# Three later feed-forward parts: eleven chunk pairs by seven products, the last four by token blocks, and some low parts on GpSimd

## The chip, the core and the metric

The kernel runs on one core of a Trainium2 chip. TensorE (PE) multiplies, VectorE (DVE), ScalarE (ACT) and GpSimd (POOL) do the elementwise work, and SyncE (SP) issues most of the DMAs; POOL's queue issues some. The metric is the device time of one execution in microseconds (us), the median of several runs.

## The reference

Two layers over 512 tokens of width 1024. Each layer has a feed-forward part, three kinds of attention with gates (the mix), and a second feed-forward part, each followed by a layer norm:

```python
def _swiglu(x, w1, w2):
    gt, up = jnp.split(x @ w1, 2, axis=-1)
    return (jax.nn.silu(gt) * up) @ w2
...
    for l in range(DEPTH):                                   # DEPTH = 2
        x = _layer_norm(DN_ALPHA * x + 0.5 * _swiglu(x, ffn1_w1[l], ffn1_w2[l]), ln1_g[l], ln1_b[l])
        mix = _token_mix(x, w_in[l], ...)
        x = _layer_norm(DN_ALPHA * x + mix, ln2_g[l], ln2_b[l])
        x = _layer_norm(DN_ALPHA * x + 0.5 * _swiglu(x, ffn2_w1[l], ffn2_w2[l]), ln3_g[l], ln3_b[l])
    return x
```

`w1` is 1024 x 5632, `w2` is 2816 x 1024; all is float32. So there are four feed-forward parts, and the change is in their second matrix `w2`.

## The kernel before

**Split numbers.** A float32 number is held as a high part (`hi`, `sh`, `xh`: a copy in TensorE's rounded format, made by ACT) and a low part (`lo`, `sl`, `xl`: the number minus its high part, made by DVE). A product of two such numbers is three matmuls: high by high, low by high, high by low. Weights arrive by SP DMAs in `raw` buffers and are split by `wsplit` (L156).

**The second matrix, `strassen_rows` (L321).** The 2816 rows of `w2` are 22 chunks of 128 rows. Two chunks are a pair: with the two halves of the columns (512 each) and the two halves of the tokens (256 each, two blocks of 128) a pair is a product of 2 x 2 blocks, done with 7 block products where the plain way has 8. A block product is 2 token blocks x 3 matmuls of 128 x 128 by 128 x 512. Nine pairs (`NS` = 9) are done so; the last four chunks (`NTAIL`) are plain, 24 matmuls each.

- *First pass:* for each pair four of the seven products, with sums of weight blocks that the POOL queue's DMAs have added up in DRAM long before (`weight_sums`, L478, one step at a time by `sums_step`, L497: a small POOL copy that waits for a tile, then a DMA). The operands' sums of token blocks are made by DVE on the way. All eight PSUM banks accumulate.
- *Between:* ACT and DVE read the four results (`reads`, L377), and DVE adds them into the residual rows `xa` in twelve small steps (`merge`, L385), some from SBUF alone, some with an operand in PSUM.
- *Second pass:* for each pair the other three products. `second(p)` (L414) prepares a pair two ahead: the row of weights (`wrows`), the weights' sum for two pairs at a time, and `sp(p, True)` (L765), which makes `sh` (ACT) and `sl` (DVE, 128 x 768, L590) from the sums of tokens. Four such pairs of buffers exist, and five units of split weights.
- *Tail, `norm_tail` (L261):* the four plain chunks' 96 matmuls token block by token block; after each block its layer norm (`LN.steps`, L222): DVE takes the accumulators (L229), ACT the sum of squares (L232), POOL two one-column steps (L235, L236), DVE the two scalings (L234, L240). `LN.second` (L244) transposes the block and splits it for the next stage. In between the next stage's first weights are loaded and split. The next stage (`staged`, L464, or `value_rows`, L820) starts with the blocks that are done first.

PE, POOL, ACT and DVE run these stages in the order in which they are written. In the last part there is no next stage; L242 sends the result out.

Of the kernel before, what the change touches and what calls it, by code (L numbers as in the profile page):

```python
# [18 lines left out]
P = 128  # L19
# [45 lines left out]
def body(tc, a, out, depth=DEPTH):  # L65
# [89 lines left out]

    def wsplit(raw, n=KD, step=None):  # L156
        hi, lo = unit()
        step = step or n
        for i in range(0, n, step):
            c = slice(i, i + step)  # L160
            nc.scalar.activation(hi[:, c], raw[:, c], AF.Copy)  # L161
            nc.vector.tensor_tensor(lo[:, c], raw[:, c], hi[:, c].bitcast(F32), op=OP.subtract)  # L162
        return hi, lo

    def wcols(w, c0, step=None):

        r = wraw()
        nc.sync.dma_start(r, w.rearrange("(k p) f -> p k f", p=P)[:, :, c0:c0 + P])
        return wsplit(r, step=step)

# [29 lines left out]
    class LN:  # L200
# [20 lines left out]

        def steps(self, acc, tb, tpl):  # L222
            x = self.xa[tb]
            st = stats[tb]
            junk = tpl.tile([P, D], BF, name="junk", bufs=2)
            u = tpl.tile([P, D], F32, name="u", bufs=2)
            hs = [slice(0, 512), slice(512, 1024)]
            for hf, c in enumerate(hs):
                nc.vector.scalar_tensor_tensor(x[:, c], acc[hf], self.scale, x[:, c], op0=OP.mult, op1=OP.add,  # L229
                                               accum_out=st[:, hf:hf + 1])  # L230
# [3 lines left out]
            nc.vector.scalar_tensor_tensor(u, x, st[:, 2:3], self.G, op0=OP.add, op1=OP.mult)  # L234
            nc.gpsimd.tensor_scalar(st[:, 4:5], st[:, 3:4], 1.0 / D, EPS / ALPHA ** 2, op0=OP.mult, op1=OP.add)  # L235
            nc.gpsimd.tensor_tensor(st[:, 5:6], st[:, 4:5], mhalf, op=OP.pow)  # L236
            yield
            for c in hs:
                y = u if self.last else x
                nc.vector.scalar_tensor_tensor(y[:, c], u[:, c], st[:, 5:6], self.B[:, c], op0=OP.mult, op1=OP.add)  # L240
                if self.last:
                    nc.sync.dma_start(out[tb * P:(tb + 1) * P, c], y[:, c])  # L242
# [17 lines left out]

    def norm_tail(accs, half, ln, nxt, early=False):  # L261


        wts = []

        def load(n):
            for _ in range(n if nxt else 0):
                wts.append(nxt(len(wts)))

        when = [2, 1, 1, 0, 0] if early else [1, 1, 1, 0, 1]  # L270
        load(when.pop(0))
        for tb in range(NB):
            half(tb, 0)
            if tb >= 2:
                ln.second(tb - 2)
            half(tb, 1)
            if tb == NB - 1:
                next(st, 0)
            st = ln.steps(accs[tb], tb, nx.pool)
            next(st)  # L280
            next(st)
            if tb != NB - 2:
                next(st, 0)
            load(when.pop(0))
        return wts, {0: lambda: ln.second(NB - 2), 2: lambda: ln.second(NB - 1)}

# [34 lines left out]
    def strassen_rows(w2, ts, first, order, enter, sp, plain, clear, nxt, tmp, early):  # L321
# [48 lines left out]
        p1, p6, p7, p5 = (a1[i:i + 2] for i in (0, 4, 2, 6))  # L370
        a2 = acc8()
        accs = [[a2[4 * (tb // 2) + 2 * hf + tb % 2] for hf in range(2)] for tb in range(NB)]
        tt, stt = nc.vector.tensor_tensor, nc.vector.scalar_tensor_tensor
# [11 lines left out]
        def merge(b):  # L385
# [6 lines left out]
            yield stt(xb[:, c1], u3[b], -sc, xb[:, c1], op0=OP.mult, op1=OP.add)  # L392
# [18 lines left out]

        merges = chain([merge(0), merge(1)])

        def second(p):  # L414
            if p < NS:
                ready.append((weights(p), sp(p, True)))
# [3 lines left out]
        second(1)  # L420
        for p in range(NS):
            (uc, d, dc), (sh, sl) = ready.popleft()
            prods = [(0, 1, uc, lo4), (1, 0, uc, hi4), (2, 2, d, dc)]
            for i, j, w, c in prods[2:] + prods[:2] if p and dc.start == 4 or p == NS - 1 else prods:
                for b in range(2):
                    mm(a2[2 * i + b], (sh[:, j], sl[:, j]), w, b, c, p == 0, False)
            second(p + 2)
            for _ in range(12 // NS + (p < 12 % NS)):
                next(merges)
            if p >= NS - 2:  # L430
                prep(2)
        for _ in range(2 * NS, KF - NTAIL):
# [31 lines left out]
    def staged(wts, pend):  # L464

        pts = [ps(name="pj") for _ in wts]
        for i, (o, w) in enumerate(zip(pts, wts)):
            proj(o, w, halves[0])
            if i in pend:
                pend[i]()  # L470
        for o, w in zip(pts, wts):
            proj(o, w, halves[1])
        return pts

    NTAIL = 4
    sums = deque()

    def weight_sums(w2, ns):  # L478


        ts = dram.tile([P, ns, 2048], F32, name="ts", tag=f"ts{ns}", bufs=3 if ns == 9 else 1)
        n = 3

        def step(g, i):
            c = slice(n * g, n * g + n)
            v = w2[2 * n * g * P:2 * n * (g + 1) * P].rearrange("(q two p) f -> two p q f", two=2, p=P)
            b11, b12, b21, b22 = (v[j][:, :, 512 * k:512 * k + 512] for j in range(2) for k in range(2))
# [4 lines left out]
        for r in (range(6), range(6, 8)):  # L492
            for g in range(ns // n):
                sums.extend(lambda g=g, i=i: step(g, i) for i in r)
        return ts

    def sums_step(t, psum=False):  # L497
        if sums:
            if psum:
                nc.scalar.activation(pace2, t[0:64, 0:1], AF.Copy)  # L500
                t = pace2
            nc.gpsimd.tensor_copy(pace[0:64], t[0:64, 0:1])
            sums.popleft()()
# [69 lines left out]
    def ffn(l, w1, w2, which, xap, xa, wts, pend, done_prev, last, nxt, ts):  # L573
# [13 lines left out]

        def parts(hi, lo, x):
            nc.scalar.activation(hi, x, AF.Copy)  # L589
            nc.vector.tensor_tensor(lo, x, hi.bitcast(F32), op=OP.subtract)  # L590
# [208 lines left out]
    def mix_first(l):  # L799
# [4 lines left out]

        def step(j):
            if not t:
# [13 lines left out]
    def value_rows(w, pend):  # L820


        pts = []
        for tb in range(NB):
            o = ps(name="vr", shape=(P, 4, P))
            pts.append(o)
            t = slice(tb * P, (tb + 1) * P)
            for k in range(KD):
# [3 lines left out]
                nc.tensor.matmul(o, xh[:, k, t], lo, start=False, stop=k == KD - 1)  # L832
            if tb < 2:
                pend[2 * tb]()
        return pts

    def mix(l, wts, pend, done_ffn, xap, xa, nxt):
# [16 lines left out]
        v4 = at.tile([P, NB, 4, P], F32, name="v4")  # L854
        for tb in range(NB):
            nc.scalar.activation(v4[:, tb], pts[tb], AF.Copy)
# [848 lines left out]
    for l in range(depth):  # L1705
        fin = l == depth - 1
        wts, pend, done, xap, xa = ffn(l, a["ffn1_w1"][l], a["ffn1_w2"][l], 0, xap, xa, wts, pend, done, False,
                                       mix_first(l), ts.pop(0))
        ts += [weight_sums(w, 9) for w in [a["ffn2_w2"][l]] + ([] if fin else [a["ffn1_w2"][l + 1]])]
        wts, pend, done, xap, xa = mix(l, wts, pend, done, xap, xa, ffn_first(a["ffn2_w1"][l]))  # L1710
        assert not sums
        wts, pend, done, xap, xa = ffn(l, a["ffn2_w1"][l], a["ffn2_w2"][l], 2, xap, xa, wts, pend, done, fin,
# [31 lines left out]
```

## Time and profile before

| | us |
|---|---|
| median of three runs (lowest to highest) | 2446.52 (2444.11 to 2447.5) |
| the profiled execution, its own time | 2443.86 |
| its span, from first to last instruction | 2442.1 |
| TensorE busy in it | 2422.3 (99%) |
| DVE busy | 1837.0 (75%) |
| ACT busy | 1186.2 (49%) |
| POOL busy | 474.9 (19%) |

The granted TensorE clock is 0.999 of full speed. In the timeline rows below, the first number is the start, the second the duration, both in us; then engine, source line, operation, output and inputs, shapes, and how many are merged (x2), and in brackets the idle time before it with what ended it. Durations of operations that follow at once overlap a little: a DVE subtract shown with 1.22 us is followed by the next after 1.14. In the chain rows the numbers are start and duration of a piece.

The four second matrices start at 242.7, 1116.2, 1453.4 and 2327 us: layer 0 first and second part, layer 1 first and second part. "Later parts" are the last three.

### The profile page before, as it was taken

The page shows a single profiled execution, that of the slowest core. Times are in us where ns is not written, and L with a number is a line of the kernel's source. Part 1 is how long each engine was busy: PE and PEld are TensorE (multiplying, and loading weights), DVE is VectorE, ACT ScalarE, POOL GpSimd, SP SyncE. Part 2 cuts the span into 40 slices and gives each one's busy share as a digit, 9 for nine tenths or more (in the row PEclk, how much of TensorE's full clock was granted, in tenths as well). Part 3 has the DMA queues.
Part 4 walks back from the last instruction along what each step waited for, and adds up shares of the span by engine and source line. Part 5 has one row for each costly group of instructions (what it writes and reads, how often), then busy time and mean ns, then how long its engine had stood idle before and what let it go on. Part 6 is the DMA issues. An engine that isn't in the chain of part 4 may idle for free.

```text
span 2442.1 us, 40840 instructions
## 1 busy us (share of the span) xinstructions
PE 2422.3 (99%) x15475; PEld 2145.0 (88%) x15475; DVE 1837.0 (75%) x3625; ACT 1186.2 (49%) x2292; POOL 474.9 (19%) x670
## 2 busy tenths in 40 slices
PE   9999999999999999999999999999999999999998
PEld 8999887788888899998899998877888888999987
DVE  6899985687653469999879999666776443799997
ACT  4444644576632334445534456455666322344463
POOL 4332400144422200004000004012443100000040
PEclk9999999999999999999999999999999999999999
DMA  7888754666499942336533347446665833333373
GB/s 206 224 223 214 259 161 125 173 152 154 108 256 270 250 124 78 104 106 215 186 111 104 104 133 250 146 137 167 158 138 118 254 100 103 104 96 105 106 243 121
DMA packets 422581, 390.02 MB, mean 160 GB/s; under 512 B 20472, under 2 KB 352392, under 8 KB 422384
## 3 DMA queue, kind: packets, MB, share of 16 engines
q1 hardware_dynamic: 385792, 287.00, 39.7%
q0 software_dynamic: 36592, 100.41, 16.7%
q8 instruction: 122, 2.00, 0.3%
q14 instruction: 75, 0.61, 0.1%
HBM read 360.02 MB, written 93.38 MB: 186 GB/s over the span
## 4 chain that ended last, share of the span: by engine, by line
PE 96%; DVE 2%; ACT 1%; issue 1%; DMA 1%; SPq 0%; DVEq 0%; POOLq 0%; ACTq 0%; POOL 0%
PE acc L331 17%; PE pg L644 17%; PE pu L644 8%; PE pj L182 5%; PE pj L183 5%; PE pj L184 5%; PE pv L644 4%; PE gate L182 3%; PE gate L184 3%; PE gate L183 3%; PE brp L184 2%; PE brp L182 2%; PE brp L183 2%; PE sN L1253 2%; PE ptN L1295 1%; PE po L1314 1%
## 5 line engine op out<-in xcount | busy, mean ns | idle before, releaser
L162 DVE TENSOR_TENSOR lo<-raw,hi 128x1024 fp32r<-128x1024 f32 (+2 forms) x262 | 300.0, 1158 | 254.1 <-ACT hi L161 253.4
L161 ACT ACTIVATE hi<-raw 128x1024 fp32r<-128x1024 f32 (+2 forms) x262 | 259.1, 1004 | 328.7 <-DMA raw<-in_w_gate_dram 76.6
L182 PE MATMUL pj<-xh,hi 128*128 128x512 f32 (+1 forms) x720 | 266.9, 371 | 0.1
L184 PE MATMUL pj<-xh,lo 128*128 128x512 f32 (+1 forms) x720 | 254.7, 354 | 0.0
L183 PE MATMUL pj<-xl,hi 128*128 128x512 f32 (+1 forms) x720 | 254.5, 354 | 0.0
L644 PE MATMUL pg<-xh,lo 128*128 128x256 f32 x864 | 244.5, 283 | 0.0
L644 PE MATMUL pg<-xl,hi 128*128 128x256 f32 x864 | 244.5, 283 | 0.0
L644 PE MATMUL pg<-xh,hi 128*128 128x256 f32 x864 | 244.5, 283 | 0.0
L352 POOL COPY pace<-sh 64x1 f32<-64x1 f32 x16 | 95.5, 5967 | 677.2 <-ACT sh L589 677.2
L331 PE MATMUL acc<-hi,sh 128*128 128x512 f32 x568 | 221.5, 390 | 0.0
L331 PE MATMUL acc<-lo,sh 128*128 128x512 f32 x568 | 221.0, 389 | 0.0
L331 PE MATMUL acc<-hi,sl 128*128 128x512 f32 x568 | 221.0, 389 | 0.0
L541 DVE TENSOR_TENSOR lo<-ws,hi 128x1024 fp32r<-128x1024 f32 x144 | 175.0, 1216 | 0.0
L644 PEld LDWEIGHTS pg<-xh,hi 128*128 128x128 f32 x864 | 165.9, 192 | 0.2
L644 PEld LDWEIGHTS pg<-xl,hi 128*128 128x128 f32 x864 | 165.9, 192 | 0.2
L644 PEld LDWEIGHTS pg<-xh,lo 128*128 128x128 f32 x864 | 165.9, 192 | 0.0
L644 PE MATMUL pu<-th,hi 128*128 128x256 f32 x576 | 163.0, 283 | 0.0
L644 PE MATMUL pu<-tl,hi 128*128 128x256 f32 x576 | 163.0, 283 | 0.0
L644 PE MATMUL pu<-th,lo 128*128 128x256 f32 x576 | 163.0, 283 | 0.0
L184 PEld LDWEIGHTS pj<-xh,lo 128*128 128x128 f32 x720 | 136.2, 189 | 19.6
L538 ACT ACTIVATE hi<-ws 128x1024 fp32r<-128x1024 f32 x144 | 144.1, 1048 | 16.3 <-DVE ws L523 15.3
L182 PEld LDWEIGHTS pj<-xh,hi 128*128 128x128 f32 x720 | 136.6, 190 | 15.3 <-issue 3.1
(365 smaller groups left out, 6632.5 us busy)
## 6 DMA issues: line engine op xcount, KB each, us to landing
raw<-in_ffn_w_dram SPq DMA_DIRECT2D x228, 512.0 KB, 4.3
ts<-in_ffn_w_dram POOLq DMA_DIRECT2D x72, 768.0 KB, 8.0
raw<-in_w_in_dram SPq DMA_DIRECT2D x56, 512.0 KB, 4.1
raw<-ts SPq DMA_DIRECT2D x52, 512.0 KB, 3.9
raw<-in_w_gate_dram SPq DMA_DIRECT2D x48, 512.0 KB, 5.8
ts<-ts POOLq DMA_DIRECT2D x24, 768.0 KB, 10.0
x_sp<-xa POOLq DMA_DIRECT2D x24, 512.0 KB, 6.2
ks<-hl SPq DMA_DIRECT2D x96, 128.0 KB, 2.4
```

The source lines that it names most:

```text
L161: nc.scalar.activation(hi[:, c], raw[:, c], AF.Copy)
L162: nc.vector.tensor_tensor(lo[:, c], raw[:, c], hi[:, c].bitcast(F32), op=OP.subtract)
L182: nc.tensor.matmul(o, hi[:, k], vh, start=first, stop=False)
L183: nc.tensor.matmul(o, hi[:, k], vl, start=False, stop=False)
L184: nc.tensor.matmul(o, lo[:, k], vh, start=False, stop=last)
L331: nc.tensor.matmul(o, xx[:, t], ww[:, c], start=first and i == 0, stop=last and i == 2)
L352: nc.gpsimd.tensor_copy(pace[0:64], sp(min(p + 1, NS - 1))[0][0:64, 0, 0:1].bitcast(F32))
L538: nc.scalar.activation(t[0], x, AF.Copy)
L541: nc.vector.tensor_tensor(t[1], x, t[0].bitcast(F32), op=OP.subtract)
L644: nc.tensor.matmul(o, wx, vx, start=first and k == 0 and i == 0, stop=k == 3 and i == 2, skip_group_check=True)
L1253: nc.tensor.matmul(o[:, 0:nb].rearrange("p k b j -> p (k b j)"), q, kx[:, 2 * b0:2 * (b0 + nb)].rearrange("p a b -> p (a b)"), start=i == ...
L1295: nc.tensor.transpose(pt[:, k, br], p[:, k, br], ident)
```

## The change

- The three later parts do all eleven pairs by seven products (`weight_sums(w, KF // 2)`); the first keeps nine and four plain chunks. The sums of the eleven need eight DMA steps more in each of the three; 16 of the steps wait until the next part's first matrix (`keep`).
- In the later parts the second pass does seven pairs as before, of pair 7 the two products of the first token half, and then pairs 7 to 10 by token blocks, in the order 2, 3, 0, 1: blocks 2 and 3 have one product of each pair (12 matmuls a block), blocks 0 and 1 two (18). Six PSUM banks are used in place of eight, with another assignment, and the merges come in another order; blocks 2 and 3 need only one accumulator in L229.
- `sl` in every second pass (the first part's too) is made by POOL. In the tails of the later parts the low parts of the next weights are made by POOL (but for the first load ahead of a mix).
- `norm_tail` gets the order of blocks, puts the norm of block 0 behind the first half of block 1, and the next stage starts with tokens 256 to 511. In the last part, ACT scales and POOL adds for blocks 2 and 3 in place of L240.

```diff
-    def wsplit(raw, n=KD, step=None):
+    def wsplit(raw, n=KD, step=None, eng=None):
...
-            nc.vector.tensor_tensor(lo[:, c], raw[:, c], hi[:, c].bitcast(F32), op=OP.subtract)
+            (eng or nc.vector).tensor_tensor(lo[:, c], raw[:, c], hi[:, c].bitcast(F32), op=OP.subtract)
...
             for c in hs:
                 y = u if self.last else x
-                nc.vector.scalar_tensor_tensor(y[:, c], u[:, c], st[:, 5:6], self.B[:, c], op0=OP.mult, op1=OP.add)
+                if eng:
+                    nc.scalar.activation(u[:, c], u[:, c], AF.Copy, scale=st[:, 5:6])
+                    eng.tensor_tensor(y[:, c], u[:, c], self.B[:, c], op=OP.add)
+                else:
+                    nc.vector.scalar_tensor_tensor(y[:, c], u[:, c], st[:, 5:6], self.B[:, c], op0=OP.mult, op1=OP.add)
...
-    def norm_tail(accs, half, ln, nxt, early=False):
+    def norm_tail(accs, half, ln, nxt, early=False, seq=tuple(range(NB))):
...
-                wts.append(nxt(len(wts)))
+                wts.append(nxt(len(wts), nc.gpsimd if seq[0] and (wts or not early) else None))
-        when = [2, 1, 1, 0, 0] if early else [1, 1, 1, 0, 1]
+        when = ([2, 0, 1, 1, 0] if early else [1, 1, 1, 1, 0]) if seq[0] else [2, 1, 1, 0, 0] if early else [1, 1, 1, 0, 1]
...
+        late = seq[0] > 0
+        for n, tb in enumerate(seq):
             half(tb, 0)
-            if tb >= 2:
-                ln.second(tb - 2)
+            if n >= 2:
+                ln.second(seq[n - 2])
+            if n == NB - 1 and late:
+                run(st, 2)
             half(tb, 1)
...
-        a2 = acc8()
+        whole = 2 * NS == KF
+        Q = 4 if whole else 0
+        a2 = [ps(name="acc") for _ in range(6)] if whole else acc8()
+        if whole:
+            a2 = a2[2:] + a2[:2]
...
+        def merge_b(b):
+            xb = ln.xa[2 + b]
+            yield stt(xb[:, c0], u3[b], sc, xb[:, c0], op0=OP.mult, op1=OP.add)
+            yield tt(u3[b], p5[b], u3[b], op=OP.add)
+            yield stt(xb[:, c1], u3[b], -sc, xb[:, c1], op0=OP.mult, op1=OP.add, accum_out=stats[2 + b][:, 1:2])
+            yield tt(u2[b], p5[b], u2[b], op=OP.add)
+        def merge_a(b):
+            xa = ln.xa[b]
+            yield stt(xa[:, c0], v1[b], sc, xa[:, c0], op0=OP.mult, op1=OP.add)
+            yield stt(xa[:, c1], u2[b], -sc, xa[:, c1], op0=OP.mult, op1=OP.add)
...
-        for p in range(NS):
+        for p in range(NS - Q):
...
+        if whole:
+            (u, d, dc), x = ready[0]
+            d2 = small(NS - 2)
+            shs = [sp(NS - 2, True), sp(NS - 1, True)]
+            ready.append(((wrows(w2, 2 * NS - 3), d2, lo4), shs[0]))
+            for b in range(2):
+                for i, c in ((0, lo4), (1, hi4)):
+                    mm(a2[2 * i + b], (x[0][:, 1 - i], x[1][:, 1 - i]), u, b, c, False, False)
+            ready[0] = (None, d, dc), x
+            ready.append(((wrows(w2, 2 * NS - 1), d2, hi4), shs[1]))
...
+            def half(tb, hf):
+                if accs[tb][hf] is None:
+                    return
+                for n, ((uc, d, dc), (sh, sl)) in enumerate(ready):
+                    j, w, c = (2, d, dc) if tb >= 2 else ((1, uc, lo4), (0, uc, hi4))[hf]
+                    if w:
+                        mm(accs[tb][hf], (sh[:, j], sl[:, j]), w, tb % 2, c, False, n == Q - 1)
+            wts, pend = norm_tail(accs, half, ln, nxt, early, (2, 3, 0, 1))
...
         for i, (o, w) in enumerate(zip(pts, wts)):
-            proj(o, w, halves[0])
-            if i in pend:
+            proj(o, w, halves[half], range(4))
+            if half and i in pend:
+                pend[i]()
+            proj(o, w, halves[half], range(4, KD))
+            if not half and i in pend:
                 pend[i]()
...
             if second:
                 hi, lo = pair()
-                parts(hi[:, 0:3], lo[:, 0:3], halves_of(p)[:, 1:4])
+                parts(hi[:, 0:3], lo[:, 0:3], halves_of(p)[:, 1:4], nc.gpsimd)
                 return hi, lo
...
-        ts += [weight_sums(w, 9) for w in [a["ffn2_w2"][l]] + ([] if fin else [a["ffn1_w2"][l + 1]])]
+        ts += [weight_sums(w, KF // 2) for w in [a["ffn2_w2"][l]] + ([] if fin else [a["ffn1_w2"][l + 1]])]
+        keep[0] = 0 if fin else 16
```

More of the change, by code (lines that the diff above doesn't have):

```diff
@@ L220, in first, with steps @@
                 pass
-        def steps(self, acc, tb, tpl):
+        def steps(self, acc, tb, tpl, eng=None):
             x = self.xa[tb]
@@ L267, in load, with run @@
             for _ in range(n if nxt else 0):
-                wts.append(nxt(len(wts)))
-        when = [2, 1, 1, 0, 0] if early else [1, 1, 1, 0, 1]
+                wts.append(nxt(len(wts), nc.gpsimd if seq[0] and (wts or not early) else None))
+        when = ([2, 0, 1, 1, 0] if early else [1, 1, 1, 1, 0]) if seq[0] else [2, 1, 1, 0, 0] if early else [1, 1, 1, 0, 1]
         load(when.pop(0))
-        for tb in range(NB):
+        def run(st, n):
+            for _ in range(n):
+                next(st, 0)
+        late = seq[0] > 0
+        for n, tb in enumerate(seq):
             half(tb, 0)
-            if tb >= 2:
-                ln.second(tb - 2)
+            if n >= 2:
+                ln.second(seq[n - 2])
+            if n == NB - 1 and late:
+                run(st, 2)
             half(tb, 1)
[L277 to L283, printed above, removed]
+            ahead = st if n == NB - 1 else iter(())
+            if not ln.last:
+                run(ahead, 1)
+            st = ln.steps(accs[tb], tb, nx.pool, nc.gpsimd if ln.last and n < NB - 2 else None)
+            if n == NB - 2:
+                run(st, 0 if late else 2)
+            else:
+                run(st, 2)
+                run(ahead, 1)
+                run(st, 1)
             load(when.pop(0))
-        return wts, {0: lambda: ln.second(NB - 2), 2: lambda: ln.second(NB - 1)}
+        return wts, {int(late): lambda: ln.second(seq[2]), 2 + late: lambda: ln.second(seq[3]), "first": seq[0] // 2}
     def rows_ln(nk, wload, sh, sl, ln, nmain, clear, nxt):
@@ L370, in strassen_rows @@
         p1, p6, p7, p5 = (a1[i:i + 2] for i in (0, 4, 2, 6))
-        a2 = acc8()
-        accs = [[a2[4 * (tb // 2) + 2 * hf + tb % 2] for hf in range(2)] for tb in range(NB)]
+        whole = 2 * NS == KF
[3 more added lines that the diff above has]
+            a2 = a2[2:] + a2[:2]
+        accs = [[a2[4 * (tb // 2) + 2 * hf + tb % 2] if tb < 2 or not (whole and hf) else None for hf in range(2)]
+                for tb in range(NB)]
         tt, stt = nc.vector.tensor_tensor, nc.vector.scalar_tensor_tensor
@@ L410, in prep @@
                 rest.append((k, plain(k), wrows(w2, k)))
-        merges = chain([merge(0), merge(1)])
+        merges = chain([merge_b(0), merge_b(1), merge_a(0), merge_a(1)] if whole else [merge(0), merge(1)])
         def second(p):
-            if p < NS:
+            if p < NS - Q // 2:
                 ready.append((weights(p), sp(p, True)))
@@ L427, in strassen_rows @@
             second(p + 2)
-            for _ in range(12 // NS + (p < 12 % NS)):
+            for _ in range(12 // (NS - Q) + (p < 12 % (NS - Q))):
                 next(merges)
@@ L492, in weight_sums @@
         for r in (range(6), range(6, 8)):
-            for g in range(ns // n):
+            for g in range((ns + 2) // 3):
                 sums.extend(lambda g=g, i=i: step(g, i) for i in r)
@@ L497, in sums_step @@
     def sums_step(t, psum=False):
-        if sums:
+        if len(sums) > keep[0]:
             if psum:
@@ L820, in value_rows @@
     def value_rows(w, pend):
-        pts = []
-        for tb in range(NB):
+        pts = [None] * NB
+        half = 2 * pend.get("first", 0)
+        for n in range(NB):
+            tb = (n + half) % NB
             o = ps(name="vr", shape=(P, 4, P))
-            pts.append(o)
+            pts[tb] = o
             t = slice(tb * P, (tb + 1) * P)
@@ L832, in value_rows @@
                 nc.tensor.matmul(o, xh[:, k, t], lo, start=False, stop=k == KD - 1)
-            if tb < 2:
-                pend[2 * tb]()
+                if half and k == 2 and n in (1, 2):
+                    pend[2 * n - 1]()
+            if n < 2 and not half:
+                pend[2 * n]()
         return pts
@@ L854, in mix @@
         v4 = at.tile([P, NB, 4, P], F32, name="v4")
-        for tb in range(NB):
+        for n in range(NB):
+            tb = (n + 2 * pend.get("first", 0)) % NB
             nc.scalar.activation(v4[:, tb], pts[tb], AF.Copy)
```

55 lines of the change are left out of this document (34 added, 21 removed).

## The prediction

> **What bounds the kernel now.** I read the page first (busy time, the chain that ended last), then the chain in order of time, then the busy time by stage, then the timelines of DVE, ACT and POOL in one second pass and one tail.
>
> ```profile
> span 2442.1 us, 40840 instructions
> PE 2422.3 (99%) x15475; PEld 2145.0 (88%) x15475; DVE 1837.0 (75%) x3625; ACT 1186.2 (49%) x2292; POOL 474.9 (19%) x670
> PE 96%; DVE 2%; ACT 1%; issue 1%; DMA 1%; SPq 0%; DVEq 0%; POOLq 0%; ACTq 0%; POOL 0%
> ```
>
> ```profile
> 242.66 99.32 PE acc L331 x438
> 1116.18 99.31 PE acc L331 x438
> 1216.37 5.46 PE acc L331 x24
> 1222.70 2.77 PE acc L331 x12
> ```
>
> ```profile
> 291.70:328.40 36.70, 36.70 (x163) 30.41 (x162) 33.39 (x40) 21.82 (x26) 0.00 (x0) 1.00 0.59 181
> 1165.10:1201.90 36.80, 36.80 (x164) 30.50 (x163) 33.49 (x40) 22.09 (x26) 0.00 (x0) 1.00 0.57 179
> 1201.90:1225.30 23.40, 23.40 (x112) 19.51 (x112) 18.08 (x31) 8.17 (x13) 2.22 (x6) 1.00 0.51 146
> ```
>
> TensorE is the bound: 99% busy, 96% of the chain, and 438 products of the second matrix follow one another without a hole, one every 99.31/438 = 0.2267 us. So a product taken away is worth 0.2267 us, as long as TensorE keeps going. The window rows (columns: stretch, sum, PE, PEld, DVE, ACT, POOL, clock, DMA share, GB/s) show how near the next engine is: in a second pass (36.8 us) DVE is busy 33.4 to 33.5 us, 91%, POOL not at all.
>
> **What is taken away.** A pair by 7 products costs 42 matmuls (24 first pass, 18 second), two plain chunks 48. Two more pairs in each of three parts: 3 x 12 x 0.2267 = 8.2 us. That is the whole gain; the order by token blocks moves matmuls and removes none (7 x 18 + 12 + 12 + 12 + 18 + 18 = 11 x 18). The transposes stay.
>
> **What is moved to POOL, and the port.** In every second pass, the unchanged first part's too, POOL makes `sl` (128x768, two inputs in SBUF) instead of DVE, and in the tails of the later parts most `lo` of the next weights. The trace has no wide POOL operation with two inputs, but it shows what happens when POOL reads SBUF beside DVE operations of that kind:
>
> ```profile
> 1130.13 21.74 POOL L352 COPY pace<-sh 64x1 f32<-64x1 f32 x1 [3.16 <-ACT sh L589]
> ...
> 1150.28 1.21 DVE L348 TENSOR_TENSOR lo<-raw,hi 128x1024 fp32r<-128x1024 f32 x1
> 1151.41 0.41 DVE L604 TENSOR_TENSOR ha<-ha,s 128x256 f32<-128x256 f32 x1
> 1152.35 0.45 DVE L590 TENSOR_TENSOR sl<-ha,sh 128x256 fp32r<-128x256 f32 x1 [0.53 <-ACT sh L589]
> ```
>
> ```profile
> 519.27 1.23 DVE L162 TENSOR_TENSOR lo<-raw,hi 128x1024 fp32r<-128x1024 f32 x1
> 521.65 0.49 DVE L1276 TENSOR_TENSOR stN<-stN 128x4 f32<-128x4 f32 x1 [0.43 <-ACT p L1271]
> ...
> 519.28 2.17 POOL L1392 TENSOR_SCALAR_AFFINE_SELECT nckd<-nck 128x1024 f32<-128x1024 f32 x1 [7.88 <-DVE stN L1265]
> 521.45 0.68 POOL L1098 TENSOR_SCALAR p<-p,stF 128x512 f32<-128x512 f32 x1
> ...
> L1392 POOL TENSOR_SCALAR_AFFINE_SELECT nckd<-nck x8: 1087/1096/2167, 448.0 to 1825.0; 128x1024 f32<-128x1024 f32 x8
> ```
>
> A copy of one column took 21.74 us and ended at 1151.87, just when DVE, after subtracts without a hole, stood idle for 0.53 us. At 519.28 a POOL operation that needs 1.09 us alone (the least of its eight) took 2.17, the 1.23 of the DVE subtract longer; and at 521.65 a DVE operation on four columns took 0.49 us, until POOL's of 0.68 was over. So one holds the way to SBUF and the other waits for its end, and back-to-back DVE subtracts leave POOL out until DVE idles or takes an operand from PSUM. (The Trainium skill, "SBUF — State Buffer", section Who interferes with whom, says that a DVE instruction with two SBUF inputs contends with a GpSimd instruction that reads SBUF. The rows above agree.)
>
> **POOL's price.** From 0.68 us for 512 columns and 1.09 for 1024: 0.8 ns a column and 0.27 us fixed, for one input. Lower bound: the second input costs nothing, 0.87 us for 768 columns. Upper bound: the whole doubles, 2.2 us for 1024 and 1.7 for 768. I take double the column price and the fixed part once: 1.5 us for 768 and 1.9 for 1024, nearer the upper row, since both inputs must be fetched over the way just seen. DVE needs 0.95. The Trainium skill, "GPSIMD Engine Reference", section 3.1, gives 4497 ns for a two-input fp32 operation of 2048 columns, as an estimate 1.69 us for 768; by it the sum below would be the upper one, near 2467 us; no run here shows it.
>
> **First part, end of its second pass.** All its wanted products stand, so any stall is pure loss.
>
> ```profile
> 318.39 1.23 DVE L162 TENSOR_TENSOR lo<-raw,hi 128x1024 fp32r<-128x1024 f32 x1 [2.75 <-ACT hi L161]
> 319.54 0.95 DVE L590 TENSOR_TENSOR sl<-ha,sh 128x768 fp32r<-128x768 f32 x1
> 320.40 0.69 DVE L390 SCALAR_TENSOR_TENSOR xa<-s,xa 128x512 f32<-128x512 f32 x1
> 321.01 0.68 DVE L391 SCALAR_TENSOR_TENSOR xa<-G,xa 128x512 f32<-128x512 f32 x1
> 321.61 1.29 DVE L590 TENSOR_TENSOR sl<-hb,sh 128x512 fp32r<-128x512 f32 x2
> 322.81 2.35 DVE L162 TENSOR_TENSOR lo<-raw,hi 128x1024 fp32r<-128x1024 f32 x2
> 325.09 0.68 DVE L392 SCALAR_TENSOR_TENSOR xa<-B,xa 128x512 f32<-128x512 f32 x1
> 325.69 1.28 DVE L590 TENSOR_TENSOR sl<-hb,sh 128x512 fp32r<-128x512 f32 x2
> ...
> 318.27 0.83 ACT L589 ACTIVATE sh<-ha 128x768 fp32r<-128x768 f32 x1
> 325.46 2.01 ACT L161 ACTIVATE hi<-raw 128x1024 fp32r<-128x1024 f32 x2 [2.39 <-PE acc L331]
> ```
>
> `sh` of the last pair is ready at 319.10, while DVE is inside the subtract of 318.39. Without L590 at 319.54 the rest closes up (start to start): two merges to 320.8, two `sl` of plain chunks to 322.0, two `lo` to 324.2, a merge to 324.8, two `sl` to 326.0, all from SBUF, none waiting. The first hole is there, as the next `hi` ends at 326.5. POOL's `sl` runs from 326.0 to 327.5. TensorE wants it at the second matmul of pair 8: the pass starts at 242.5 + 216 x 0.2267 = 291.5, so 291.5 + 8 x 4.08 + 0.23 = 324.4. **Stall 3.2 us** (2.5 with 0.87, 3.4 with 1.7); nothing before on DVE covers it.
>
> **Later parts, start of the second pass.**
>
> ```profile
> 1163.17 1.37 DVE L383 TENSOR_TENSOR B<-acc,G 128x512 f32<-128x512 f32 x2
> 1164.45 2.35 DVE L162 TENSOR_TENSOR lo<-raw,hi 128x1024 fp32r<-128x1024 f32 x2
> 1167.59 1.22 DVE L162 TENSOR_TENSOR lo<-raw,hi 128x1024 fp32r<-128x1024 f32 x1
> 1169.60 0.68 DVE L387 TENSOR_TENSOR G<-acc,G 128x512 f32<-128x512 f32 x1
> ...
> 1163.52 0.83 ACT L589 ACTIVATE sh<-ha 128x768 fp32r<-128x768 f32 x1
> ```
>
> The first accumulators now lie where L383 reads; it ends at 1164.54, the pass starts at 1116.0 + 49.0 = 1165.0: free, unless DVE is 0.5 us later. `sh` of pair 1 is ready at 1164.35; POOL starts with 0.1 us in hand before three `lo` (1.14 each) and the first merge (0.6, from SBUF now, since the merges were reordered). The next one reads PSUM, at 1168.5: `sl` is there at 1170.0, wanted at 1165.0 + 4.08 + 0.23 = 1169.3, 0.7 late; pair 2's follows after two `lo` and a merge (2.9) at 1174.4, wanted at 1173.4 + 0.7: 0.3 more. **+1.0** each (0.1 to 1.4).
>
> **Later parts, last four pairs.** Their `sl` must all be there for the first token block. DVE's own run of row 6, two merges, rows 7, the sums of 7 and 8 and a merge (3 x 1.14 + 3 x 0.6 = 5.2 us) begins when the weights' buffers come free and ends about 25.5 + 1.0 us into the pass; none of it lets POOL in. Then five `sl` (7.5) and three `lo` and a merge (4.0) share the way: 26.5 + 11.5 = 38.0, wanted at 7 x 4.08 + 12 x 0.2267 + 2.3 + 1.0 = 34.6. **+3.4** each (0.3 to 4.3).
>
> **Later parts, the tail.** Per token block, from the accumulator to the end of L240:
>
> ```profile
> 1207.37 0.69 DVE L229 SCALAR_TENSOR_TENSOR xa<-acc,xa 128x512 f32<-128x512 f32 x1 [2.02 <-PE acc L331]
> 1208.35 1.28 DVE L234 SCALAR_TENSOR_TENSOR u<-xa,st,G 128x1024 f32<-128x1024 f32 x1
> 1210.55 1.42 DVE L240 SCALAR_TENSOR_TENSOR xa<-u,st,B 128x512 f32<-128x512 f32 x2 [0.91 <-ACT hi L161]
> ...
> 1209.96 0.56 POOL L236 TENSOR_TENSOR st<-st,mhalf 128x1 f32<-128x1 f32 x1
> ```
>
> 4.6 us, one after the other on DVE. The tail shrinks from 96 products (21.8 us) to 60 (13.6). L236 now stands behind subtracts of 1.9 us on POOL's queue, which also hold up L234. Counted from the end of block 2's products: its L240 ends at 4.6, its transposes are wanted at 2.72 + 2.04 = 4.8, just covered. Block 3: reads until 5.4, the subtract until 6.5, L234, square, L236, L240 until 10.9; wanted at 4.8 + 0.9 + 4.1 = 9.8, 1.1 late. Block 0 follows 2.6 us of `xl`, 4.6 of its own and up to 1.9 of waiting: 20.0, wanted by the next stage at 18.1; I count half of the 1.9 late, as POOL may be done by then. **+2.0** in the two parts with a next stage (0.5 to 3). In the last part there are no weights, but two L240 stand behind the last block's L234, one of them before, in the gap that L236 left, and the POOL additions delay it: **+0.8** (0 to 1.5).
>
> **Nothing, and why.**
>
> ```profile
> ts<-in_ffn_w_dram POOLq DMA_DIRECT2D x72, 768.0 KB, 8.0
> ts<-ts POOLq DMA_DIRECT2D x24, 768.0 KB, 10.0
> ```
>
> The two pairs more in the first pass take 5.44 us each on TensorE, with the same mix of DVE work as the pairs there now. Of the sums' DMA steps there are 24 more beside these 96, each behind a POOL copy; 16 move into the next part's first matrix, where POOL has no one waiting for it. TensorE, 99% busy with the 96, covers them; without that cover a late `raw` would cost some us. On SP's queue the loads keep their order but for row 7's, now ahead of its sums, and the output's order of blocks.
>
> **Sum.** 3.2 + 3 x (-2.7 + 1.0 + 3.4) + 2 x 2.0 + 0.8 = +13.1 us. The profiled execution took 2443.9 (span 2442.1), the median of the runs is 2446.5; on it: 2459.6, say **2459**. All lower bounds: 2.5 + 3 x (-2.7 + 0.1 + 0.3) + 1.0 = -3.4, 2443. All upper: 3.4 + 3 x 3.0 + 6 + 1.5 = +20, 2466.5; a few us more if stalls add up, 2472.
>
> **Rivals.** (1) *The other side: full gain, 2438.* If POOL, once it waits, gets in between two DVE subtracts, `sl` always lands within the two pairs of lead and only the 8.2 us stay. For it: DVE is relieved of 0.95 us of about 3.7 in each 4.08. Against: the 21.74 us row. It decides at the point where POOL's wait falls under about 2 us. (2) *POOL is cheap, 2443.* The way is shut as seen, but the price is the lower row's; for it speaks only the 0.68 and 1.09 us of one input. (3) *POOL dear, 2467:* the upper sums. It differs from the forecast in size alone. That the change does not do what it says is not seen: the products are counted from the code.
>
> **Chances.** Measurement tells about 0.2% (5 us) from nothing. Forecast with (3): 0.60, its own range 2450 to 2472. (2), within 5 us: 0.18. (1): 0.22. So slower 0.60, same 0.18, faster 0.22; the range 2437 to 2472 reaches over all three, as (1) and (2) together hold too much to be left out.
>
> **What will show it.** Right: holes of TensorE, which now has none in these stretches, at pair 8 of the first part (about 324 to 327), and at the start and end of each later second pass, waiting for `sl` from POOL, with POOL `sl` spans of several us that end at a DVE hole or PSUM read. Wrong: `sl` on POOL at about 1 us or less, no holes in the acc chain, and three parts each 2.7 us shorter. A tail that waits for L240 while POOL is in `lo` proves the tail's step; one that waits for DVE alone disproves it.

## The result, and the profile after

The changed kernel takes 2474.2 us (median) against 2447.0 for the kernel before beside it: ratio 1.011, 95% interval 1.0095 to 1.0125. It is slower, as forecast, but by 27 us, where the prediction had 13 and a range that ended at 2472. The profiled execution took 2473.5 us, the one of before 2443.9.

The page, and the waits of TensorE over the whole span (columns: us in total, times, the longest; `pt` are the transposes of the norm, `vr` the next stage's first products). Lines are now those of the changed kernel: L347 was L331, L656 was L590, L231, L236, L238 and L246 were L229, L234, L236 and L240. (Experiments 4 and 7 edit the kernel before and have its lines.)

```profile
span 2471.5 us, 40988 instructions
PE 2428.2 (98%) x15439; PEld 2142.9 (87%) x15439; DVE 1878.6 (76%) x3596; ACT 1203.3 (49%) x2311; POOL 622.0 (25%) x774
```

```profile
PE acc L347 <- DVE lo L162: 14.3, 7, 5.5
PE pt L257 <- DVE xa L246: 6.3, 5, 1.7
PE vr L899 <- DVE xa L231: 0.7, 1, 0.7
```

TensorE runs 36 matmuls fewer and yet is busy 5.9 us longer; it waits 21.3 us where it did not wait before, always for DVE and never for POOL. DVE itself, relieved of its 36 `sl` and of ten `lo`, is busy 41.6 us longer than before (1878.6 for 1837.0). The view of POOL's subtracts says why the first reading, that POOL is too late, would be wrong: the list of who waited for `sl` is empty.

```profile
L656 POOL TENSOR_TENSOR sl<-ha,sh x36: 1846/2034/2896, 288.7 to 2436.7; 128x768 fp32r<-128x768 f32 x36
L656 POOL TENSOR_TENSOR sl<-hb,sh x6: 2680/2751/2831, 1209.1 to 2442.1; 128x768 fp32r<-128x768 f32 x6
its engine sat idle before it (us, times) until:
  ACT sh L655: 116.1, 39
who waited for it (us, times):
```

By stage (columns as before): the first second pass, the second part's, and its tail. DVE is busy all of the first 36.7 us; in the tail TensorE works 15.7 of 23.8 us.

```profile
295.15:331.85 36.70, 36.20 (x159) 29.49 (x158) 36.70 (x29) 21.51 (x25) 17.03 (x8) 1.00 0.54 164
1169.50:1206.30 36.80, 36.30 (x159) 29.49 (x158) 31.61 (x27) 21.86 (x25) 16.61 (x8) 1.00 0.58 181
1214.65:1238.42 23.77, 15.69 (x71) 12.65 (x71) 21.82 (x23) 7.80 (x12) 13.51 (x8) 0.93 0.50 151
```

The last part has no next stage and shows it cleanest. Timeline of DVE, then POOL, then TensorE, from the first read of its second pass to its first norm:

```profile
2407.62 1.37 DVE L402 TENSOR_TENSOR G<-s,acc 128x512 f32<-128x512 f32 x2 [2.69 <-PE acc L347]
2408.91 1.37 DVE L404 TENSOR_TENSOR B<-acc,G 128x512 f32<-128x512 f32 x2
2410.19 6.83 DVE L162 TENSOR_TENSOR lo<-raw,hi 128x1024 fp32r<-128x1024 f32 x3
...
2434.70 2.34 DVE L424 SCALAR_TENSOR_TENSOR xa<-s,xa 128x512 f32<-128x512 f32 x1
2436.96 2.33 DVE L425 SCALAR_TENSOR_TENSOR xa<-G,xa 128x512 f32<-128x512 f32 x1
...
2447.13 3.48 DVE L162 TENSOR_TENSOR lo<-raw,hi 128x1024 fp32r<-128x1024 f32 x3
...
2410.17 1.85 POOL L656 TENSOR_TENSOR sl<-ha,sh 128x768 fp32r<-128x768 f32 x1 [3.54 <-ACT sh L655]
2412.59 2.21 POOL L656 TENSOR_TENSOR sl<-ha,sh 128x768 fp32r<-128x768 f32 x1 [0.58 <-ACT sh L655]
...
2436.73 2.01 POOL L656 TENSOR_TENSOR sl<-ha,sh 128x768 fp32r<-128x768 f32 x1 [0.25 <-ACT sh L655]
2439.45 5.47 POOL L656 TENSOR_TENSOR sl<-hb,sh 128x768 fp32r<-128x768 f32 x2 [0.71 <-ACT sh L655]
...
2448.40 0.77 PE L347 MATMUL acc<-lo,sh 128*128 128x512 f32 x1 [3.38 <-DVE lo L162]
```

Three `lo` that take 3.5 us by themselves (the row at 2447.13) take 6.8 beside two `sl`; a merge of 0.68 us takes 2.3. So POOL gets its turn between two back-to-back DVE subtracts, after at most the one that runs, and DVE then stands for the 1.85 us. At the first token block TensorE waits 3.4 us, from 2445.02 on, for a `lo` that DVE has not come to; POOL's last `sl` had ended at 2444.92. The matmul behind the hole takes 0.77 us where the others take 0.39: the second loss, the granted clock (last section).

In the tails POOL's `lo` of the next weights does the same to the norm. DVE and POOL in part 2's tail, then DVE in part 3's:

```profile
1225.48 3.53 DVE L246 SCALAR_TENSOR_TENSOR xa<-u,st,B 128x512 f32<-128x512 f32 x2 [0.92 <-ACT hi L161]
...
1225.55 2.92 POOL L162 TENSOR_TENSOR lo<-raw,hi 128x1024 fp32r<-128x1024 f32 x1
...
1571.80 1.42 DVE L246 SCALAR_TENSOR_TENSOR xa<-u,st,B 128x512 f32<-128x512 f32 x2 [2.11 <-POOL st L238]
```

L246, 1.42 us by itself, takes 3.4 to 3.5 us beside a `lo` of POOL, three times. Once, at 1571.80, it is POOL's own step that is late: it stood behind a `lo`, and DVE waited 2.11 us for it instead of 0.9.

Against before, from the start of one second matrix to the next (profiled executions; 2.7 us are saved in each later part):

| us longer than before | to the first | to part 2's | to part 3's | to the last | to the end | span |
|---|---|---|---|---|---|---|
| changed kernel | 3.5 | 1.0 | 8.8 | 10.8 | 5.4 | 29.4 |
| `sl` on DVE (below) | 3.0 | 0.4 | 1.3 | 3.8 | -1.3 | 7.2 |
| nothing on POOL (below) | 1.5 | 0.1 | 0.6 | 5.4 | -0.3 | 7.3 |

The first column is not of the change. In kernels whose work up to there is the same, the first second matrix starts anywhere from 242.4 to 246.2 us. The profile of before had one of the quick starts (what goes with them is in the last section); by the medians the difference is 27.2.

### The profile page after: what moved, and what is told of

It reads as the page before. It is cut to its first block, busy times and chain, and to the rows that moved or that the text cites. A ratio compares the mean times of both kernels' runs of the same rounds, so it can differ in the third digit from the quotient of the medians.

```text
span 2471.5 us, 40988 instructions
## 1 busy us (share of the span) xinstructions
PE 2428.2 (98%) x15439; PEld 2142.9 (87%) x15439; DVE 1878.6 (76%) x3596; ACT 1203.3 (49%) x2311; POOL 622.0 (25%) x774
## 5 line engine op out<-in xcount | busy, mean ns | idle before, releaser
L162 DVE TENSOR_TENSOR lo<-raw,hi 128x1024 fp32r<-128x1024 f32 (+2 forms) x255 | 321.1, 1274 | 243.8 <-ACT hi L161 234.5
L347 PE MATMUL acc<-lo,sh 128*128 128x512 f32 x556 | 220.0, 396 | 14.3 <-DVE lo L162 14.3
L347 PE MATMUL acc<-hi,sh 128*128 128x512 f32 x556 | 219.3, 394 | 0.0
L347 PE MATMUL acc<-hi,sl 128*128 128x512 f32 x556 | 218.5, 393 | 0.0
L604 ACT ACTIVATE hi<-ws 128x1024 fp32r<-128x1024 f32 x144 | 144.0, 1048 | 16.3 <-DVE ws L589 15.3
```

What stands on the lines that cost most here:

```text
L162: (eng or nc.vector).tensor_tensor(lo[:, c], raw[:, c], hi[:, c].bitcast(F32), op=OP.subtract)
L347: nc.tensor.matmul(o, xx[:, t], ww[:, c], start=first and i == 0, stop=last and i == 2)
L604: nc.scalar.activation(t[0], x, AF.Copy)
```

## The experiments

**1. `sl` back on DVE.**

```
-                parts(hi[:, 0:3], lo[:, 0:3], halves_of(p)[:, 1:4], nc.gpsimd)
+                parts(hi[:, 0:3], lo[:, 0:3], halves_of(p)[:, 1:4])
```

> As the changed kernel, but the second pass's sl (128x768) is made by DVE again; the tails' lo and additions stay on POOL. Theory A (a POOL subtract holds the way to SBUF for its 1.85 us and DVE, which needs 0.95 for the same work, waits): the hole of 3.4 us at the start of the tails of ffn1 and the last part goes, with the half-clock stretch behind it (1.5 us), and that of 5.5 us shrinks to about 2; three parts, so about 15 us less than the changed kernel: 2459 (2453 to 2464). Theory B (the shorter tail, 60 products for 96, is what cannot cover the merges and the norm, whoever makes sl): the holes stay, 2470 to 2476. Theory C (half clock at the start of the program and extra DMAs, not POOL): 2470 to 2476 as well, with the second matrix of the first part still starting 3.4 us late.

Measured 2450.3 us (before beside it 2447.8; ratio 1.0012, 1.0002 to 1.0021). 24 of the 27 us are gone with this one edit; the holes at the start of the tails are gone altogether, more than Theory A had asked for. The same stretch of the last part on DVE:

```profile
2392.09 1.37 DVE L402 TENSOR_TENSOR G<-s,acc 128x512 f32<-128x512 f32 x2 [1.82 <-PE acc L347]
...
2415.51 0.69 DVE L424 SCALAR_TENSOR_TENSOR xa<-s,xa 128x512 f32<-128x512 f32 x1
2416.11 0.68 DVE L425 SCALAR_TENSOR_TENSOR xa<-G,xa 128x512 f32<-128x512 f32 x1
...
2427.57 1.23 DVE L162 TENSOR_TENSOR lo<-raw,hi 128x1024 fp32r<-128x1024 f32 x1 [0.42 <-ACT hi L161]
```

From L402 to the end of the last `lo` DVE needs 36.7 us here and 43.0 in the changed kernel, though ten `sl` of 0.87 us (start to start) were taken from it: 6.3 + 8.7 = 15.0 us of waiting, 1.5 for each `sl` (DVE idles 0.7 us of the first stretch and 0.1 of the second). What was moved off DVE came back 1.7 times.

**2. The tails' `lo` and the last part's additions back on DVE, `sl` on POOL.**

```
-                wts.append(nxt(len(wts), nc.gpsimd if seq[0] and (wts or not early) else None))
+                wts.append(nxt(len(wts), None))
-            st = ln.steps(accs[tb], tb, nx.pool, nc.gpsimd if ln.last and n < NB - 2 else None)
+            st = ln.steps(accs[tb], tb, nx.pool)
```

> As the changed kernel, but all lo of the next stage's weights and the last part's additions are on DVE; sl stays on POOL. Theory A: the lo that stood ahead of the merge (3.4 us on POOL) goes, so the hole of 5.5 us falls to the 3.4 us that the parts without it show, and the holes of 1.0 to 1.7 us later in the two tails go in part, as DVE now has 1.14 us more for each lo: about 5 to 8 us less, 2467 (2463 to 2472). Theory B: the same 2474 or more, as DVE has more to do in the same 13.6 us (2474 to 2480).

Measured 2471.7 (before 2447.8; 1.0095, 1.008 to 1.011), at the upper end of Theory A's range and just below Theory B's. The hole of 5.5 us did fall to the 3.4 of the other parts, as A had it, but the holes later in the tails only changed their place. By the medians, what POOL does in the tails costs 2.5 us with `sl` on POOL; the intervals of the two kernels against before overlap, so this is not shown. With `sl` on DVE (kernel 1 against the next, ten runs each) it gains 2.6, by the means 1.8.

**3. Nothing moved to POOL** (the edits of 1 and 2 together).

> As the changed kernel, with nothing moved to POOL: eleven pairs by 7 products and token blocks, all subtracts and the norm on DVE. Theory A: the 36 products saved (8.2 us) show, less what the short tail costs DVE: 2444 (2438 to 2452), holes at the start of the tails under 1 us. Theory B: the tail of 13.6 us cannot hold the norm of four blocks (4.6 us each on DVE) and the next weights, so holes of 3 us and more stay in each part: 2458 to 2470.

Measured 2452.9 (before 2447.8; 1.0020, 1.0010 to 1.0029): just above Theory A's range and well below Theory B's. With no wide POOL subtract anywhere, the 36 products saved bring nothing. The last part's second matrix is 2.7 us shorter, as counted, but in the third part TensorE waits 5.1 us (waits from 1540 to 1575; then DVE's timeline there):

```profile
PE vr L899 <- DVE xa L231: 2.8, 1, 2.8
PE pt L257 <- DVE xa L246: 2.3, 2, 1.3
```

```profile
1548.84 2.49 DVE L882 TENSOR_TENSOR lo<-raw,hi 128x512 fp32r<-128x512 f32 x4
...
1557.62 1.23 DVE L162 TENSOR_TENSOR lo<-raw,hi 128x1024 fp32r<-128x1024 f32 x1 [1.18 <-ACT hi L161]
...
1567.33 0.68 DVE L231 SCALAR_TENSOR_TENSOR xa<-acc,xa 128x512 f32<-128x512 f32 x1
```

From 1548.84 to 1567.33 DVE has the norm of two blocks, the next weights and `xl`: 18.5 us, 3.0 of them idle, against a tail of 13.6 us of products. Before, 96 products (21.8 us) lay over it. In this tail DVE, not TensorE, is the bound, and a product saved there saves nothing.

**4. `sl` on POOL in the kernel before.**

```
-                parts(hi[:, 0:3], lo[:, 0:3], halves_of(p)[:, 1:4])
+                parts(hi[:, 0:3], lo[:, 0:3], halves_of(p)[:, 1:4], nc.gpsimd)
```

> The kernel before with one edit: the second pass's sl (nine pairs by 7 products in all four parts) made by POOL. By the prediction's step (POOL is left out by back-to-back subtracts, so that the last pair's sl is 3.2 us late in the second pass): 3.2 us in each of four parts and the start of the pass, 2459 to 2463. Theory A (POOL gets its turn between two DVE subtracts and then DVE waits 1.85 us for it): sl in time, holes of 0.5 us at most each, 2447 to 2451, and DVE's merges and subtracts beside an sl take 2.3 us and more.

Measured 2452.3 (before 2447.8; 1.0021, 1.0011 to 1.0030). All four second matrices, the unchanged first part's too, are 1.0 us longer, with one hole of 0.5 us each near the start of the second pass and none at pair 8: Theory A's 0.5 and not the prediction's 3.2, though the time is 1.3 us over Theory A's range. From one matmul's start to the next the hole costs 0.66 us; three later starts in the pass are 0.04 to 0.11 us late each, which is most of the rest of the 1.0. So `sl` on POOL alone costs 4.5 us and pairs with blocks alone 5.2, but both together (experiment 2) 23.9. I read this so: with nine pairs the lateness of DVE runs out in the four plain chunks, while in the changed kernel the first token block wants all of it at once. No run shows that part by itself.

**5. A subtract that nobody uses.** Kernel 1, and for each `sl`:

```
+                nc.gpsimd.tensor_tensor(lo[:, 3:4], halves_of(p)[:, 1:2], hi[:, 0:1].bitcast(F32), op=OP.subtract)
```

> As the changed kernel with sl made by DVE (2450), and one more subtract on POOL for every sl, 128x256, whose result nobody uses. Theory A (DVE is held for as long as POOL's subtract lasts, about 0.7 us each, eleven times a pass): DVE's merges and subtracts beside it are 0.5 to 0.7 us longer, DVE comes 4 to 7 us later to the end of the pass, of which the slack takes about 3; holes of 1 to 4 us at the start of the three tails and 1.5 us of half clock behind some: 2454 to 2468. Theory B (the loss of the changed kernel is that POOL's own sl is late for TensorE): no hole, 2448 to 2452.

Measured 2463.4 (before 2447.0; 1.0067, 1.0052 to 1.0083), 14 us over kernel 1 (each against its own before). POOL's extra subtracts; then DVE's timeline around 1207 us:

```profile
L836 POOL TENSOR_TENSOR sl<-ha,sh x36: 734/1104/1826, 288.6 to 2431.0; 128x256 fp32r<-128x256 f32 x36
```

```profile
1206.74 0.68 DVE L424 SCALAR_TENSOR_TENSOR xa<-s,xa 128x512 f32<-128x512 f32 x1
1207.34 1.75 DVE L162 TENSOR_TENSOR lo<-raw,hi 128x1024 fp32r<-128x1024 f32 x1
1209.02 1.50 DVE L656 TENSOR_TENSOR sl<-ha,sh 128x768 fp32r<-128x768 f32 x1
```

The subtracts of DVE beside them are 0.54 us longer each, and TensorE again waits, for DVE's own `sl`, 3.1 us at the end of the second part's pass. Half of the 14 us are not holes: TensorE is busy 7.0 us longer than in kernel 1 (2426.7 for 2419.7), mostly at half clock. Every wanted `sl` is DVE's, and what POOL makes in the tails is the same as in kernel 1: this is the sharpest evidence that the loss is DVE's time, not the lateness of what POOL makes.

**6. `sl` of pair 7 and on by DVE, the seven before by POOL** (`nc.gpsimd if p < 7 else None`).

> As the changed kernel, but sl of the pairs from number 7 on is made by DVE; the seven before stay on POOL. Theory A (each sl on POOL costs DVE 1.85 us of waiting for 0.87 saved, and it is the sum that makes the hole, 6.3 us over ten of them): about two thirds of it, 4.2 us, less the slack of 2.9: holes of 1 to 1.5 us at the start of each tail without half clock; 2458 to 2464. Theory B (it is the last four, wanted all at once by the first token block): the holes at the start of the tails go, 2451 to 2455.

Measured 2461.3 (before 2447.0; 1.0056, 1.0043 to 1.0070), the time of Theory A. The place was not as either had it: nothing at the start of the tails, but 3.6 and 3.0 us at their second step, waiting for the norm (L246), as DVE comes late into the tail. Four of eleven `sl` taken off POOL bring 13 of the 24.6 us that all eleven bring; the seven before them still cost 11.8. So it is the sum over the pass that counts, not the last four alone.

**7. The row that misled.** In the kernel before, the one-column copy of line 352 as a subtract of two inputs:

```
-                nc.gpsimd.tensor_copy(pace[0:64], sp(min(p + 1, NS - 1))[0][0:64, 0, 0:1].bitcast(F32))
+                y = sp(min(p + 1, NS - 1))[0][0:64, 0, 0:1].bitcast(F32)
+                nc.gpsimd.tensor_tensor(pace[0:64], y, y, op=OP.subtract)
```

> The kernel before, with one edit: the one-column POOL copy that paces the first matrices (line 352, 64x1) is a subtract of two inputs of the same 64x1. In the kernel before, 4 of its 16 take about 22 us, beside back-to-back DVE subtracts. Theory D (what is left out is a copy; an operation with two inputs gets its turn between two DVE operations, as sl did): all 16 take under 2.5 us, the median of x16 stays near 0.6 us, and DVE operations beside them are up to 0.5 us longer. Theory E (what is left out is whatever POOL does there, in a stretch where every DVE operation reads SBUF twice): 4 of 16 still take about 22 us. Time the same in both, 2444 to 2451.

2448.6 us in one execution; Theory D fell: four still take about 22 us. Then, in the same stretch of the kernel before, the 128x768 `sl` of the first pass (`parts(..., nc.gpsimd if n == 3 else None)` in `s_split`):

> The kernel before, with the 128x768 sl of the first pass (beside the back-to-back DVE subtracts where the one-column copy took 22 us) made by POOL. Theory E (in that stretch POOL is left out whatever it does): sl spans of 4 us and more, TensorE waiting for sl from POOL in every pair, until DVE runs dry and lets POOL in: holes of some us in each of 36 pairs, 2500 or more. Theory G (a wide subtract gets its turn at the end of the DVE operation that runs, here as in the second pass; only the one-column operation is left out): sl spans of 1.85 to 3.1 us, DVE operations beside them up to 1.85 us longer, TensorE waiting for DVE's lo or for POOL by one DVE operation at a time; 2455 to 2500.

2449.2 us in one execution, 6 us less than Theory G's least. The first kernel's copy, then from the second kernel POOL's `sl`, the copy and DVE's L604 (min, median, max in ns):

```profile
L353 POOL TENSOR_TENSOR pace<-sh x16: 392/577/22033, 255.7 to 2368.9; 64x1 f32<-64x1 f32 x16
```

```profile
L590 POOL TENSOR_TENSOR sl<-s,sh x28: 1868/1882/2149, 253.2 to 2371.9; 128x768 fp32r<-128x768 f32 x28
...
L352 POOL COPY pace<-sh x16: 362/378/399, 259.6 to 2362.7; 64x1 f32<-64x1 f32 x16
...
L604 DVE TENSOR_TENSOR ha<-ha,s x28: 424/2074/2079, 252.3 to 2372.0; 128x256 f32<-128x256 f32 x28
```

Not one of 28 wide subtracts is left out, in a stretch where DVE is busy 43.5 of 44 us; DVE's next operation waits instead (2.07 us for 0.42), and even the copies, now behind an `sl`, take 0.4 us. So neither its kind (copy or subtract) nor the stretch alone is what holds one small operation per part for 22 us; its width by itself was not tried, and the cause stays open. How it ended is on record: in the kernel before, ACT's next `sh` waits 3.52 us for the copy, and DVE, which needs that `sh`, runs dry just as it ends.

**8. Candidates.** Eleven pairs in the second and last part only (the third as before), `sl` and all `lo` on DVE, the last part's additions on POOL, and the loads of the second part's tail moved:

```
-        when = ([2, 0, 1, 1, 0] if early else [1, 1, 1, 1, 0]) if seq[0] else [2, 1, 1, 0, 0] if early else [1, 1, 1, 0, 1]
+        when = [1, 0, 1, 1, 1] if seq[0] else [2, 1, 1, 0, 0] if early else [1, 1, 1, 0, 1]
...
-        ts += [weight_sums(w, KF // 2) for w in [a["ffn2_w2"][l]] + ([] if fin else [a["ffn1_w2"][l + 1]])]
+        ts += [weight_sums(w, n) for w, n in [(a["ffn2_w2"][l], KF // 2)] + ([] if fin else [(a["ffn1_w2"][l + 1], 9)])]
```

> A candidate against both kernels: eleven pairs by 7 products and token blocks only in the second and the last part (the third as before: nine pairs, four plain chunks), sl and the tails' lo on DVE, the lo of the second part's tail one block later, POOL only for the last part's additions. Theory A (the saved products show wherever DVE has the time for the tail, as in the last part, 2.7 us shorter with sl on DVE): 2.7 us less in the last part, less 1.4 at its end, and 1 to 2.7 less in the second: 2442 to 2446, just under the kernel before. Theory F (the tail of 60 products costs about what the 12 products save): 2446 to 2450, no difference.

2446.7 (before 2447.0; 0.9997, 0.9988 to 1.0005): no difference, Theory F. Then `[1, 0, 1, 2, 0]`, with the fourth `lo` on POOL (first) and on DVE (second):

> As the candidate with eleven pairs in the second and the last part, but the fourth lo of the second part's tail is made by POOL, one block earlier: beside DVE's xl and first additions, which read PSUM. Theory A (POOL costs DVE nothing where DVE has an input in PSUM): the hole of 1.8 us in the next stage goes, no DVE operation is longer, 1 to 2.5 us less than that candidate: 2444 to 2446, faster than the kernel before by 0.05 to 0.1%. Theory F (the tail is at its limit, whoever makes the lo): 2446 to 2448.

> As the last kernel (eleven pairs in the second and the last part, the fourth lo of the second part's tail one block earlier), with that lo on DVE and not on POOL. Theory A (POOL's lo held DVE's lo for 1.6 us, so that xl came late): DVE's lo at that place takes 1.2 us for 2.75, the hole in front of the next stage falls from 2.4 to about 0.8 us and the half clock behind it goes; 2 to 3 us less than that kernel, 2444 to 2446. Theory F (the tail is at its limit): the same 2447.

2447.4 (before 2447.8; 0.9994, 0.9985 to 1.0003) and 2445.8 (before 2447.4; 0.9992, 0.9983 to 1.0001). Neither is distinguishable from the kernel before, nor the two from each other. DVE and POOL with the fourth `lo` on POOL, then DVE with it on DVE:

```profile
1224.17 1.28 DVE L260 TENSOR_TENSOR xl<-pt,xh 128x512 fp32r<-128x512 f32 x2
1225.37 2.75 DVE L162 TENSOR_TENSOR lo<-raw,hi 128x1024 fp32r<-128x1024 f32 x1
...
1224.65 2.39 POOL L162 TENSOR_TENSOR lo<-raw,hi 128x1024 fp32r<-128x1024 f32 x1 [2.98 <-ACT hi L161]
```

```profile
1221.55 2.35 DVE L162 TENSOR_TENSOR lo<-raw,hi 128x1024 fp32r<-128x1024 f32 x2
```

POOL's `lo` leaves `xl` alone, which reads PSUM, and holds the DVE `lo` behind it by 1.5 us. But on DVE both `lo` stand ahead of the second `xl` and take 2.35 us there: the hole is 2.0 us for 2.4, not the 0.8 expected, and the half clock behind it stays. The second time lies in Theory A's range, but not by Theory A's mechanism.

## Why the prediction was off

*Right.* The gain: 2.7 us a part, as the last part shows with `sl` on DVE. That the first pass, the further sums and the queues cost nothing: in kernel 1, which has them all, the list of TensorE's waits has no matmul of a second matrix. The places came out too: TensorE's holes lie at the start and at the end of each later second pass and in the tails, and a pass's start costs 1.0 (0.5 us of hole, in kernel 4 as well). But the prediction had TensorE wait there for POOL's `sl`, and every one of these holes waits for DVE. So it is in good part luck that the direction came out, and luck that two terms, +1.0 and +3.4, met a loss of the same size.

*The step that failed* is "back-to-back DVE subtracts leave POOL out until DVE idles or takes an operand from PSUM". It was read from one copy of 21.74 us, and experiment 7 shows that this copy speaks for no wide operation. The way is shared as quoted, but the wait falls on DVE as much as on POOL. (The Trainium skill, "SBUF — State Buffer", section Who interferes with whom, calls the port pair that DVE and GpSimd share an exclusive lock, and says that issue order, not the shape of the operation, decides who blocks. The rows of experiment 7 agree, 2.07 us for 0.42, all but that of the small copy.) The 42 `sl` of the changed kernel took 1.85 to 2.90 us each, and in the last part's pass ten of them ran while DVE was busy 42.9 of 43.0 us. From this step came the first part's 3.2 us, measured at 1.0 and in another place, and the method of the other terms: lateness of POOL's results in place of DVE's own. In no run does TensorE wait for POOL.

*Terms mis-sized.* POOL's price: 1.5 us taken, at most 1.7; it is 1.85 at least (1.26 for 512 columns, 2.33 for 1024), so the bound from one-input rows was no bound. The estimate of 1.69 that the prediction worked out from the Trainium skill, "GPSIMD Engine Reference", section 3.1, was the closer one, and still low. The last four pairs: +3.4, at most 4.3; measured holes of 3.4 us (5.5 in part 2) and 1.7 of half clock behind each, with DVE 6.3 us late in the last part. The tails: +2.0, at most 3; TensorE waited 2.6 us in part 2 and 4.4 in part 3, and again at half clock. That term was worked out as the delay of one chain of a block, with the norm's POOL step behind a `lo`; that happened once (2.11 us at 1571.80), while three times POOL's `lo` held L246 itself for 2 us more, and DVE's whole load in 13.6 us was the bound even without POOL (kernel 3). The last part's end: +0.8, at most 1.5; measured 1.8, but 2.4 with the additions on DVE (kernel 3) and 1.4 in kernel 1, so in these profiles the additions on POOL do help there.

*Left out altogether:* the half clock behind a hole. And the rival of a full gain took POOL's getting in between as free for DVE: its mechanism was true, its time was not.

*What stays open:* of the 29.4 us between the two profiles, 21.7 are TensorE's idle time, 1.8 the end. The remaining 5.9, longer busy, are -8.2 for the products and up to 10 for the half clock, the start's included; the last 4 stay open. Matmuls beside holes, whose ends are modelled, may be part of them.

## To carry to other kernels

Here, moving an operation with two SBUF inputs from DVE to POOL took from DVE what it saved and more (15.0 us for 8.7), as DVE's other work reads SBUF twice: count POOL's whole duration against DVE, and relief only where DVE reads PSUM or idles. Products saved in a stretch that covers another engine's work are worth only what that engine has to spare: add up its load against the shorter cover before counting them. One starved instruction is no law; look for a row of the same width first.

## What the runs showed of the hardware that was not expected

The granted clock falls to half on a fixed raster. In the changed kernel three of its half stretches begin at 1219.66, 1564.41 and 1581.47 us, 101 and 5 times 3.413 us apart. Cut along that raster (columns as in the stage rows; the changed kernel, then kernel 1, then the kernel with POOL's `sl` in the first pass):

```profile
1212.84:1216.25 3.41, 1.81 (x8) 1.15 (x7) 3.41 (x4) 1.93 (x2) 2.93 (x2) 1.00 0.63 182
1216.25:1219.66 3.41, 0.00 (x0) 0.00 (x0) 3.41 (x2) 0.00 (x0) 2.18 (x1) 1.00 0.55 160
1219.66:1223.07 3.41, 2.90 (x7) 2.32 (x8) 3.38 (x6) 0.00 (x0) 0.00 (x0) 0.50 0.41 154
1561.00:1564.41 3.41, 0.38 (x2) 0.34 (x3) 3.41 (x5) 0.43 (x1) 0.00 (x0) 1.00 0.25 56
1564.41:1567.82 3.41, 3.41 (x10) 2.63 (x9) 3.41 (x5) 1.15 (x2) 0.49 (x1) 0.50 0.83 264
1578.06:1581.47 3.41, 0.74 (x5) 0.50 (x6) 3.41 (x3) 2.55 (x5) 3.41 (x3) 1.00 0.57 154
1581.47:1584.88 3.41, 3.41 (x11) 2.83 (x12) 3.41 (x7) 0.79 (x2) 2.24 (x2) 0.50 0.41 41
```

```profile
1563.79:1567.20 3.41, 1.42 (x10) 1.14 (x11) 3.41 (x4) 1.93 (x5) 3.41 (x3) 1.00 0.49 140
1567.20:1570.61 3.41, 3.41 (x10) 2.67 (x9) 3.20 (x8) 1.80 (x3) 1.57 (x2) 0.50 0.48 62
```

```profile
836.56:839.97 3.41, 1.61 (x8) 0.99 (x6) 1.81 (x3) 0.00 (x0) 2.09 (x3) 1.00 0.33 40
839.97:843.38 3.41, 3.34 (x14) 2.74 (x15) 2.51 (x5) 1.56 (x3) 0.22 (x1) 1.00 1.12 214
```

A slot at whole clock in which TensorE is busy 1.42 us or less is followed by one at half clock; after 1.61 or 1.81 it stays whole. Along the same raster in the other profiles, from 10 us on, the busiest slot that half clock follows for lack of work has 1.44 us (the last candidate, from 1221.23), and the least busy one that it does not follow has 1.60 (experiment 5, from 2450.93). Two short holes do it, as at 1563.79, where 2.0 us of holes of 1.7 and 1.0 us lie in the slot. (The Trainium skill, "TensorE: Matmul & The Clock Gate", section Part 1, gives a free-running window of 3413 ns, which agrees, and an idle window as the cause; here a slot 40% busy was enough.) One thing is not explained: most profiles, but neither that of before nor that of the last candidate, have half clock for 3.4 or 6.8 us somewhere from 38 to 45 us, behind slots without any hole. The two without it have the earliest starts of the first second matrix, 242.5 and 242.4 us; those with 3.4 us of it start at 244.0 to 245.6, those with 6.8 at 245.6 to 246.2. So most of the first column of the table above, 3.5 us for the changed kernel, goes with these 6.8 us at half clock.
